# Splitting fp32 weights in two: every fourth low part from an accumulating DMA

## The chip, the core and the metric

The kernel runs on one core of a Trainium2 chip. The core has five engines with a queue of instructions each: TensorE (PE, matrix products), VectorE (DVE), ScalarE (ACT), GpSimd (POOL) and SyncE (SP, used here to issue DMAs). They meet only through semaphores. On-chip memory (SBUF) has 128 partitions; matrix products land in PSUM. Sixteen DMA engines move data between the chip's main memory and SBUF; SP, ACT and POOL can all issue transfers to them.

The metric is the device time of one execution in microseconds (us), the median over runs. The profile is of one execution of its own.

## The reference, cut to what matters

Two layers of an encoder, all in float32, on 256 positions of width 2048. Layer 0 mixes by pooling and attention, layer 1 by a matrix memory (mLSTM); each is followed by a gated feed-forward network with a convolution over positions:

```
for layer in range(DEPTH):
    h = rms_norm(x, norm_mix[layer])
    mixed = ...   # projections of h, pooling | attention, or mLSTM, output projection
    x = x + mixed
    x = x + conv_ffn(rms_norm(x, norm_ffn[layer]), w_up[layer], ..., w_down[layer])

def conv_ffn(x, w_up, conv_w, conv_b, w_down):
    u = x @ w_up                       # 2048 x 11264
    u = c[0] * up[:, :-2] + c[1] * up[:, 1:-1] + c[2] * up[:, 2:] + conv_b
    gate, val = jnp.split(u, 2, axis=-1)
    return (jax.nn.silu(gate) * val) @ w_down   # 5632 x 2048
```

Nearly all the work is products of activations with large weights, each weight used once.

## The kernel before, in words

All weights are laid out on the host as 768 chunks of 128 partitions x 1024 fp32 (512 KB) in the order in which they are used: 48 for the projections into layer 0's mixer, 32 for its output projection (chunks 48 to 79), 264 for the first feed-forward network (80 to 343), 160 for layer 1's mixer (344 to 503), 264 for the second feed-forward network.

TensorE multiplies in a fast format (`F32R`) that keeps fewer bits than fp32. To keep the accuracy, each operand is held as a high part, rounded to that format, and a low part, the rest; a product is three matmuls: high x high, low x high and high x low. `Stream` brings the weights. `load` (line 73) takes a buffer of the pool `wraw` (tag `w`, six buffers) and issues a DMA on SP. `split` (line 81) takes a buffer of the pool `wsplit` (tag `hl`, four buffers, each holding both parts), lets ScalarE cast the chunk into the high part (line 86) and VectorE subtract the high part from the chunk for the low part (line 87). `ahead` (line 91) runs loads `la` chunks and splits `sa` chunks ahead of the chunk that TensorE uses, 5 and 2 here; `next` hands a split chunk to the matmuls. A buffer comes free when its last reader is done: a raw one after the subtraction, a split one after TensorE's last matmul on the chunk.

`stat_group` (line 273) makes one group: 16 or fewer tiles of the inner dimension, four to a chunk, each tile with two matmuls of 512 columns (both parts of the activations against the high part) and two of 256 columns (the low part), all through line 188. In a feed-forward layer `up` makes a group of four chunks for each of 44 column tiles. The group leaves PSUM by a copy on ScalarE (line 321) and an addition on VectorE (322), then goes through a multiply on POOL (821), the convolution and the gate on ScalarE and VectorE (825 to 834). After some of these (4, then 8 each time) `down` makes eight groups of one or two chunks, and POOL adds each into `x` (842). PSUM holds two groups at a time.

What sets the order: TensorE's instructions stay as written in the mixers and in the last down stage; attention heads and the like are woven between projection matmuls by the list `Weave`. On the other engines, and outside the parts marked `manual_schedule`, a planner with its own model of durations orders each engine's queue and inserts the waits. An engine works its queue strictly in order, so an instruction that waits holds all behind it.

At the start the eight pieces of `x` and the first chunks are issued in turn on SP (lines 174 to 177), and the first projection (`kproj`) runs with `st.sa` at 1.

Of the kernel before, what the change touches and what calls it, by code (L numbers as in the profile page):

```python
# [9 lines left out]
F32 = mybir.dt.float32  # L10
F32R = mybir.dt.float32r
AF = mybir.ActivationFunctionType
ALU = mybir.AluOpType
# [3 lines left out]
P = 128  # L17
# [16 lines left out]
CH = 8  # L34
# [29 lines left out]
class Stream:  # L64
# [16 lines left out]
    def split(self):  # L81
        i = self.n_split
        w, n = self.w.pop(i)
        hl = self.spool.tile([P, 2, CH * P], F32R, tag="hl", name=f"hl{i}")
        for c in range(0, CH * P, n):
            self.nc.scalar.copy(hl[:, 0, c : c + n], w[:, c : c + n])  # L86
            self.nc.vector.tensor_sub(hl[:, 1, c : c + n], w[:, c : c + n], hl[:, 0, c : c + n].bitcast(F32))  # L87
        self.hl[i] = hl
        self.n_split += 1

    def ahead(self, i, split=None):
        n = len(self.srcs)
        while self.n_load < min(n, i + self.la + 1):
            if self.n_load >= self.n_split + self.la - self.sa + 1:
                self.split()
            self.load()
        while self.n_split < min(n, i + (self.sa if split is None else split) + 1):
            self.split()
# [54 lines left out]
def trunk(ctx: ExitStack, tc: tile.TileContext, xT, call, catt, cml, wgate, weights, out):  # L153
    nc = tc.nc
    v, a, g, pe = nc.vector, nc.scalar, nc.gpsimd, nc.tensor

    def pool(name, bufs, **kw):
        return ctx.enter_context(tc.tile_pool(name=name, bufs=bufs, **kw))
# [1 line left out]
    cp = pool("const", 1)  # L160
    xp = pool("xres", 1)
    actp = pool("act", 1)
    wp = pool("wraw", 6)
    sp = pool("wsplit", 4)
    smp = pool("small", 2)
    sm1 = pool("small1", 1)
    mmp = pool("mm", 2, space=PSUM)
# [2 lines left out]
    cst = cp.tile([P, NC_ALL], F32, tag="call", name="cst")  # L170
    xg = xp.tile([P, NG + KT * S], F32, tag="x", name="x")
    x = xg[:, NG:].rearrange("p (k s) -> p k s", k=KT)
    st = Stream(nc, wp, sp, weights, 5, 2)
    for i in range(8):
        c0, c1 = NG + 2 * i * S if i else 0, NG + 2 * (i + 1) * S
        nc.sync.dma_start(xg[:, c0:c1], xT[:, c0:c1])
        st.n_load < 5 and st.load(2 if i == 0 else 1)

    wv = Weave()
    ident = cst[:, C_ID : C_ID + P]  # L180
# [115 lines left out]
    def mov_group(act, name, width=512, before=None, after=None):  # L296

        ps = mmp.tile([P, 2, width], F32, tag="mm", name=name)
        per = CH * P // width
        hl = None  # L300
        for k in range(KT):
            if k % per == 0:
                before and before(k)
                hl = st.next()
                after and after(k)
            src = act(k)
            c = (k % per) * width
            for t in range(2):
                xh, xl = src[:, 0, t * P : t * P + P], src[:, 1, t * P : t * P + P]
                o = ps[:, t, :]  # L310
                first, last = k == 0 and (width == 512 or t == 0), k == KT - 1 and (width == 512 or t == 1)
                mm(o, xh, hl[:, 0, c : c + width], first, False)
                mm(o, xh, hl[:, 1, c : c + width], False, False)
                mm(o, xl, hl[:, 0, c : c + width], False, last)
            wv.tick(1.29 * width / 512)
        return ps
# [26 lines left out]
    def attention_layer(norm, nxt):  # L343
        with ExitStack() as es:
# [197 lines left out]
            with tc.manual_schedule(engines={mybir.EngineType.Activation, mybir.EngineType.DVE}):  # L542
                norm.parts(0)
                st.ahead(0, 0)
                norm.parts(1)
                st.sa = 1
                ps = mov_group(xx, "kproj", 512, ahead)
                st.sa = 2
            norm.squares(tp)
            nc.sync.dma_start(cst[:, :C_CONV], call[:, :C_CONV])  # L550
            kc = tp.tile([P, A_PW], F32, tag="rot", name="katt")
# [333 lines left out]
    norms = [Norm(0), None]  # L885
    norms[1] = Norm(1)
    attention_layer(norms[0], norms[1])
    norms.append(Norm(2))
    ffn_layer(0, norms[1], norms[2])
# [169 lines left out]
```

## Time and profile before

| | |
|---|---|
| median of 3 runs | 2225.88 us (2225.22 to 2228.11) |
| the profiled execution, its own time | 2225.61 us |
| its span in the profile | 2223.8 us |
| TensorE busy | 2213.5 us (100% of the span) |
| VectorE busy | 1695.5 us (76%) |
| ScalarE busy | 1213.1 us (55%) |
| POOL busy | 350.1 us (16%) |
| DMA engines, queue of SP | 58.5% of sixteen engines |

A row of the costliest groups reads: line, engine, operation, what it writes and reads with shapes, how often | busy time in us, mean duration in ns | idle time of the engine just before, and who ended it. A row of waits reads: the waiting engine and line, for whom, us in total, how often, the longest. A row of the timeline reads: start, duration, engine, line, operation, and in brackets the idle time before it with its releaser. A row of the stages reads: the stretch, its length, then each engine's busy time with its count of instructions, TensorE's clock as a share of full speed, the share of the DMA engines, GB/s. A row of the chain reads: start, duration, what ran.

### The profile page before, as it was taken

The page shows a single profiled execution, that of the slowest core. Times are in us where ns is not written, and L with a number is a line of the kernel's source. Part 1 is how long each engine was busy: PE and PEld are TensorE (multiplying, and loading weights), DVE is VectorE, ACT ScalarE, POOL GpSimd, SP SyncE. Part 2 cuts the span into 40 slices and gives each one's busy share as a digit, 9 for nine tenths or more (in the row PEclk, how much of TensorE's full clock was granted, in tenths as well). Part 3 has the DMA queues.
Part 4 walks back from the last instruction along what each step waited for, and adds up shares of the span by engine and source line. Part 5 has one row for each costly group of instructions (what it writes and reads, how often), then busy time and mean ns, then how long its engine had stood idle before and what let it go on. Part 6 is the DMA issues. An engine that isn't in the chain of part 4 may idle for free.

```text
span 2223.8 us, 32734 instructions
## 1 busy us (share of the span) xinstructions
PE 2213.5 (100%) x12530; PEld 1925.3 (87%) x12530; DVE 1695.5 (76%) x2099; ACT 1213.1 (55%) x1766; POOL 350.1 (16%) x277
## 2 busy tenths in 40 slices
PE   9999999999999999999999999999999999999999
PEld 7888888888888888888888889888888888888888
DVE  8677777777787777886776676778787778777776
ACT  6666565555554545565555554556555555454553
POOL 1013211312111121251000000221131211112120
PEclk9999999999999999999999999999999999999999
DMA  8545656565666656555566555665655666665664
GB/s 294 163 154 161 195 182 189 182 189 187 191 186 192 189 190 189 184 189 169 179 193 186 183 179 167 188 188 184 189 180 190 190 190 189 190 189 190 189 189 143
DMA packets 116703, 413.50 MB, mean 186 GB/s; under 512 B 12954, under 2 KB 15426, under 8 KB 116546
## 3 DMA queue, kind: packets, MB, share of 16 engines
q1 hardware_dynamic: 113616, 407.96, 58.5%
q10 hardware_dynamic: 2930, 3.45, 0.7%
q8 instruction: 98, 1.61, 0.3%
q14 instruction: 59, 0.48, 0.1%
HBM read 409.22 MB, written 2.14 MB: 185 GB/s over the span
## 4 chain that ended last, share of the span: by engine, by line
PE 97%; DVE 1%; ACT 1%; DMA 1%; issue 0%; SPq 0%; DVEq 0%
PE up L188 44%; PE dn L188 21%; PE op L188 8%; PE mk L188 4%; PE mq L188 4%; PE mo L188 4%; PE mv L188 4%; PE qproj L188 3%; PE vproj L188 1%; DMA w<-in_a_in 1%; DVE hl L87 1%; PE qk L188 1%; PE av L188 1%; PE pool L188 0%; PE ov L188 0%
## 5 line engine op out<-in xcount | busy, mean ns | idle before, releaser
L87 DVE TENSOR_TENSOR hl<-w,hl 128x1024 fp32r<-128x1024 f32 (+1 forms) x769 | 1107.4, 1441 | 298.2 <-ACT hl L86 287.3
L86 ACT CAST hl<-w 128x1024 fp32r<-128x1024 f32 (+1 forms) x769 | 807.8, 1051 | 606.6 <-PE up L188 254.3
L188 PE MATMUL up<-xx,hl 128*128 128x512 f32 (+1 forms) x5632 | 983.7, 337 | 0.0
L188 PEld LDWEIGHTS up<-xx,hl 128*128 128x128 f32 x5632 | 856.8, 188 | 125.2
L188 PE MATMUL dn<-g,hl 128*128 128x512 f32 x2784 | 488.5, 337 | 3.7 <-DVE tb_dn L322 3.7
L188 PEld LDWEIGHTS dn<-g,hl 128*128 128x128 f32 x2784 | 425.1, 189 | 66.2 <-issue 4.0
L821 POOL TENSOR_TENSOR tb_up<-tb_up,R 128x512 f32<-128x512 f32 x88 | 115.5, 1313 | 846.5 <-DVE tb_up L322 831.6
L842 POOL TENSOR_TENSOR x<-x,tb_dn 128x512 f32<-128x512 f32 x88 | 136.0, 1547 | 293.5 <-DVE tb_dn L322 293.5
L321 ACT COPY tb_dn<-dn 128x512 f32<-128x512 f32 x95 | 55.7, 586 | 135.0 <-PE dn L188 133.3
L321 ACT COPY tb_up<-up 128x512 f32<-128x512 f32 x88 | 51.6, 586 | 128.2 <-PE up L188 128.2
L322 DVE TENSOR_TENSOR tb_dn<-dn,tb_dn 128x512 f32<-128x512 f32 x95 | 65.4, 688 | 72.0 <-ACT tb_dn L321 72.0
L322 DVE TENSOR_TENSOR tb_up<-up,tb_up 128x512 f32<-128x512 f32 x88 | 60.8, 691 | 67.3 <-ACT tb_up L321 67.0
L825 ACT ACTIVATE y<-tb_up,cst 128x256 f32<-128x256 f32 x176 | 96.1, 594 | 0.0
L188 PE MATMUL op<-cat,hl 128*128 128x512 f32 (+1 forms) x512 | 92.8, 339 | 0.6 <-DVE cat L537 0.5
L188 PE MATMUL mk<-xx,hl 128*128 128x512 f32 (+1 forms) x512 | 92.5, 338 | 0.0
L188 PE MATMUL mq<-xx,hl 128*128 128x512 f32 (+1 forms) x512 | 92.0, 337 | 0.0
L188 PE MATMUL mo<-hl,xx 128*128 128x512 f32 (+1 forms) x480 | 91.6, 348 | 0.0
L188 PEld LDWEIGHTS op<-cat,hl 128*128 128x128 f32 x512 | 79.2, 188 | 12.5 <-DVE cat L537 1.0
L188 PE MATMUL op<-mcat,hl 128*128 128x512 f32 (+1 forms) x512 | 89.9, 337 | 0.0
L188 PEld LDWEIGHTS mq<-xx,hl 128*128 128x128 f32 x512 | 79.3, 188 | 11.7
L188 PE MATMUL mv<-hl,xx 128*128 128x512 f32 x384 | 89.3, 391 | 0.0
L188 PEld LDWEIGHTS mk<-xx,hl 128*128 128x128 f32 x512 | 79.1, 188 | 11.4
(219 smaller groups left out, 1560.0 us busy)
## 6 DMA issues: line engine op xcount, KB each, us to landing
w<-in_up SPq DMA_DIRECT2D x352, 512.0 KB, 4.2
w<-in_dn SPq DMA_DIRECT2D x176, 512.0 KB, 4.2
w<-in_m_in SPq DMA_DIRECT2D x128, 512.0 KB, 4.0
w<-in_a_in SPq DMA_DIRECT2D x47, 512.0 KB, 4.1
w<-in_a_out SPq DMA_DIRECT2D x32, 512.0 KB, 3.6
w<-in_m_out SPq DMA_DIRECT2D x32, 512.0 KB, 4.3
G<-gd ACTq DMA_DIRECT2D x16, 128.0 KB, 5.2
x<-in_xT SPq DMA_DIRECT2D x7, 256.0 KB, 6.9
```

Source lines behind the costliest of these rows:

```text
L86: self.nc.scalar.copy(hl[:, 0, c : c + n], w[:, c : c + n])
L87: self.nc.vector.tensor_sub(hl[:, 1, c : c + n], w[:, c : c + n], hl[:, 0, c : c + n].bitcast(F32))
L188: pe.matmul(out_, lhsT, rhs, start=start, stop=stop, skip_group_check=True)
L321: a.copy(tb, ps[:, :, 1, :])
L322: v.tensor_add(tb, ps[:, :, 0, :], tb)
L821: g.tensor_mul(u, u, bc(norm.R, 2))
L825: a.activation(y[:, j, :], u[:, j, :], AF.Identity, scale=cw(tl, 1), bias=cw(tl, 3))
L842: g.tensor_add(xs, xs, u)
```

## The change

From chunk 67 on, every fourth chunk (`i % 4 == 3`) is split in another way, 176 chunks in all. ScalarE casts the whole chunk into the high part as before. ScalarE then writes the negated high part into the place of the low part. POOL issues a DMA that reads the chunk from main memory a second time and adds it to what stands there, which leaves chunk minus high part. The raw buffer of such a chunk is free after the cast. VectorE has no part in it.

The depths change for all chunks: splits run three chunks ahead in place of two, loads six in place of five; the split pool has five buffers in place of four, and the raw pool four in place of six, which takes the same 56 KB of each partition. At the start four chunks rather than five are issued between the pieces of `x`.

```diff
@@ split
         w, n = self.w.pop(i)
         hl = self.spool.tile([P, 2, CH * P], F32R, tag="hl", name=f"hl{i}")
-        for c in range(0, CH * P, n):
+        by_dma = i % 4 == 3 and i > 64
+        if by_dma:
+            self.nc.scalar.copy(hl[:, 0], w)
+            self.nc.scalar.activation(hl[:, 1], hl[:, 0].bitcast(F32), AF.Copy, scale=-1.0)
+            self.nc.gpsimd.dma_start(hl[:, 1], self.srcs[i], accum_op=ALU.add)
+        for c in range(0, 0 if by_dma else CH * P, n):
             self.nc.scalar.copy(hl[:, 0, c : c + n], w[:, c : c + n])
             self.nc.vector.tensor_sub(hl[:, 1, c : c + n], w[:, c : c + n], hl[:, 0, c : c + n].bitcast(F32))
@@ trunk
-    wp = pool("wraw", 6)
-    sp = pool("wsplit", 4)
+    wp = pool("wraw", 4)
+    sp = pool("wsplit", 5)
...
-    st = Stream(nc, wp, sp, weights, 5, 2)
+    st = Stream(nc, wp, sp, weights, 6, 3)
...
-        st.n_load < 5 and st.load(2 if i == 0 else 1)
+        st.n_load < 4 and st.load(2 if i == 0 else 1)
@@ attention_layer
                 ps = mov_group(xx, "kproj", 512, ahead)
-                st.sa = 2
+                st.sa = 3
```

## The prediction

> **What bounds the kernel now.** I read the page first: busy times, queues, the chain of work that ended last, and the two groups that the change touches.
>
> ```profile
> span 2223.8 us, 32734 instructions
> ...
> PE 2213.5 (100%) x12530; PEld 1925.3 (87%) x12530; DVE 1695.5 (76%) x2099; ACT 1213.1 (55%) x1766; POOL 350.1 (16%) x277
> ...
> q1 hardware_dynamic: 113616, 407.96, 58.5%
> ...
> PE 97%; DVE 1%; ACT 1%; DMA 1%; issue 0%; SPq 0%; DVEq 0%
> ...
> L87 DVE TENSOR_TENSOR hl<-w,hl 128x1024 fp32r<-128x1024 f32 (+1 forms) x769 | 1107.4, 1441 | 298.2 <-ACT hl L86 287.3
> L86 ACT CAST hl<-w 128x1024 fp32r<-128x1024 f32 (+1 forms) x769 | 807.8, 1051 | 606.6 <-PE up L188 254.3
> ...
> L821 POOL TENSOR_TENSOR tb_up<-tb_up,R 128x512 f32<-128x512 f32 x88 | 115.5, 1313 | 846.5 <-DVE tb_up L322 831.6
> L842 POOL TENSOR_TENSOR x<-x,tb_dn 128x512 f32<-128x512 f32 x88 | 136.0, 1547 | 293.5 <-DVE tb_dn L322 293.5
> ...
> w<-in_up SPq DMA_DIRECT2D x352, 512.0 KB, 4.2
> ```
>
> TensorE is busy for 2213.5 of 2223.8 us, so 10.3 us is all that it ever stands idle. "Busy" in this view can hide stretching, so I looked next at the pace of its work in the chain, in two stages of the first feed-forward layer.
>
> ```profile
> 421.13 89.17 PE up L188 x512
> 510.31 44.59 PE dn L188 x256
> ```
>
> Both stages run at 174 ns per matmul (89.17/512 and 44.59/256), without a break. A chunk of weights feeds 16 matmuls, so a chunk lasts 2.787 us and an up group of four chunks 11.15 us. Last come TensorE's own waits, and stages of the run that hold them.
>
> ```profile
> PE dn L188 <- DVE tb_dn L322: 3.7, 2, 1.8
> PE wps L212 <- DVE warm L207: 1.5, 1, 1.5
> PE ptr L447 <- ACT pr L438: 0.6, 1, 0.6
> PE kproj L188 <- DVE hl L87: 0.6, 1, 0.6
> PE op L188 <- DVE cat L537: 0.5, 1, 0.5
> ```
>
> ```profile
> 0.00:30.00 30.00, 27.83 (x108) 22.21 (x109) 25.11 (x42) 23.62 (x40) 5.45 (x12) 1.00 0.93 350
> 405.00:1000.00 595.00, 594.60 (x3405) 518.67 (x3406) 466.93 (x498) 321.43 (x443) 125.50 (x90) 1.00 0.60 188
> 1482.00:1627.00 145.00, 143.17 (x823) 124.86 (x822) 115.11 (x148) 84.45 (x120) 22.80 (x18) 1.00 0.59 186
> 2131.00:2224.00 93.00, 89.59 (x515) 78.03 (x513) 63.55 (x63) 40.08 (x49) 13.86 (x10) 0.99 0.49 159
> ```
>
> A row gives the stretch, then busy time of PE, PEld, DVE, ACT and POOL, then clock, DMA share and GB/s. In the long feed-forward stretch TensorE loses 0.4 us of 595. Only once, for 0.6 us at the start, did a matmul wait for a split. The time that VectorE spends splitting is thus hidden everywhere after the start, and taking it away can win next to nothing. The question is whether what replaces it stays hidden too.
>
> **The change, part by part.** All sums go against the profiled execution's own 2225.6 us (its span plus 1.8 us around it), 0.3 us below the median of 2225.88.
>
> Removed: 176 subtractions (every fourth chunk from 67 to 767) at the mean of 1441 ns, 254 us of VectorE, which falls from 76% to 65%. Worth nothing on the path, by the waits above.
>
> Added on ScalarE: 176 passes that write the negated high part. The nearest row is the cast of the same size, 1051 ns; 185 us, ScalarE from 55% to 63%. Cover by stage: one up group.
>
> ```profile
> 699.89 0.59 ACT L321 COPY tb_up<-up 128x512 f32<-128x512 f32 x1 [1.79 <-PE up L188]
> 700.37 1.05 ACT L86 CAST hl<-w 128x1024 fp32r<-128x1024 f32 x1
> 701.28 1.29 POOL L821 TENSOR_TENSOR tb_up<-tb_up,R 128x512 f32<-128x512 f32 x1 [9.85 <-DVE tb_up L322]
> 701.46 3.47 DVE L87 TENSOR_TENSOR hl<-w,hl 128x1024 fp32r<-128x1024 f32 x2 [0.26 <-ACT hl L86]
> 703.58 1.09 ACT L825 ACTIVATE y<-tb_up,cst 128x256 f32<-128x256 f32 x2
> 706.36 0.41 ACT L831 ACTIVATE s<-y 128x256 f32<-128x256 f32 x1
> 709.15 0.40 ACT L833 CAST g<-s 128x256 fp32r<-128x256 f32 x1
> 710.98 0.58 ACT L321 COPY tb_up<-up 128x512 f32<-128x512 f32 x1 [1.44 <-PE up L188]
> ```
>
> From evacuation to evacuation there are 11.1 us; ScalarE works 0.59 + 4 x 1.05 + 1.09 + 0.41 + 0.40 = 6.7 us of them, and 7.7 us after. It fits; nothing on the path.
>
> Added on POOL and the DMA engines: 176 accumulating transfers of 512 KB. This is the term that decides. With five split buffers, the buffer of chunk j is free when TensorE has left chunk j-5, and the chunk is due four chunks later: 4 x 2.787 = 11.15 us. In the changed order of ScalarE's instructions stand the cast, the 0.40 us cast of `g`, and the negation: 1.05 + 0.40 + 1.05, and 0.3 us for handovers (0.26 us is such a gap above), 2.8 us. The transfer, from issue to landing, has the remaining 8.4 us. POOL is free to issue it: its multiply in the group above came after 9.85 us of idleness. Behind the waiting issue on POOL stands that multiply of the group just ending, or in the down stages an addition into `x`; both are due after the negation has run.
>
> How long is the transfer? No row shows one with two sources, none issued from POOL. The nearest:
>
> ```profile
> L87 DVE TENSOR_TENSOR hl<-w,hl x769: 693/1226/2317, 5.1 to 2211.4; 128x1024 fp32r<-128x1024 f32 x192, 128x512 fp32r<-128x512 f32 x1
> ...
> DMA to landing us min/median/max: 2.9/4.1/8.7
> ```
>
> ```profile
> 10.00:20.00 10.00, 9.58 (x42) 1.00 1.03 414
> ```
>
> A plain load of the same bytes lands in 2.9 to 8.7 us, 4.1 in the median. At full load the engines moved 414 GB/s, so 512 KB more to read is 1.27 us. [...] Low end 2.9; high end 8.7 + 2 x 1.27 (read and shared engines) + 1.5 = 12.7; I take 4.1 + 1.27 + 1.3 = 6.7, since most loads sit at the median. That is 1.7 us inside 8.4: hidden. If the cover is gone, each microsecond beyond 8.4 costs 176 us, up to (12.7 - 8.4) x 176 = 757 us. [...]
>
> DMA share: 176 x 2 x 1.27 = 447 us, 20% of the span, on top of 58.5%: below the 1.03 seen at full load.
>
> Moved: the depths. A raw buffer now comes back after four chunks, and the load that SP issues then has 11.15 - 1.05 - 1.44 = 8.7 us until its own split is due. At 4.2 us it is covered; the 8.7 us worst case touches a split that itself is one chunk (2.787 us) earlier than before. Nothing. For the start I looked at the chain there.
>
> ```profile
> 15.24 8.09 DMA w<-in_a_in
> ```
>
> SP's queue changes there: the fifth load waits for the first split and stands behind the last pieces of `x`, and the sixth stands behind three constant transfers, 128 + 512 + 362 KB, 2.5 us at 414 GB/s. DMA is the limit in this stretch, and TensorE loses 2.2 us of 30 already. Ends: -0.6 (the `kproj` wait goes) and +4 (those 2.5 us and one more load of 1.27); I take +1.5, as part of the 2.5 is slack.
>
> The two waits of `dn` for `tb_dn` (3.7 us) are in the short first down stage, one chunk per evacuation, where ScalarE now has two negations per layer in front of evacuations: from -3.7 to +4 x 1.05; I take 0.
>
> Outside the feed-forward layers 44 chunks go by DMA, between ScalarE work that is less regular:
>
> ```profile
> ACT hl L86 <- PE mo L188: 36.4, 21, 3.3
> ```
>
> A cast that begins 3.3 us late would miss by 1.6 us: from 0 to 44 x 1.6 = 70 us. I take 1 us, as 3.3 is the longest of 21.
>
> Sum: 2225.6 + 0 + 0 + 1.5 + 0 + 1 = 2228.1, which is +0.1%.
>
> **The rivals.** *The transfer is late* (slower). Place: the first low-part matmul of every fourth chunk; it decides from 8.4 us on. At 9.5 us it gives 1.1 x 176 = 194 us, 2420 us. For it: the 8.7 us row shows what a busy queue does, and two sources double the traffic. Against: 4.1 in the median.
>
> [...]
>
> *Scattered stalls outside the feed-forward layers.* Half of the 44 chunks miss by 1.6 us: 35 us, 2263 us. Against: no matmul there waited for a split before, but their cover shrinks.
>
> *Faster.* VectorE's relief ends the `dn` waits (3.7) and the start the `kproj` wait (0.6), with 1 us more from the deeper splits: 2220.3 us. Against: the `dn` waits end on a chain through ScalarE, which gets more work.
>
> That the change does not do what it says is excluded: the changed order has 176 DMA issues on POOL and 176 fewer subtractions.
>
> **How the numbers follow.** A measurement here tells about 0.2% (4.5 us) from no change. Hidden, as summed: 0.45, its own range 2222 to 2233, of which 0.37 within 0.2% and 0.08 slower. Late transfer 0.27, starved descriptors 0.10, scattered stalls 0.12 (0.01 of it within 0.2%), all slower. Faster rival 0.06 (0.01 within). So faster 0.05, same 0.39, slower 0.56. Though slower holds more chance in all, its cases lie far apart, and the hidden one is the likeliest: 2228 us. The range is 2220 to 2430: it leaves out about 0.02 below and about 0.15 above, the late transfers beyond 9.6 us.
>
> **What the changed profile would show.** Right: no TensorE wait for DMA in the feed-forward stages, up stages still at 89.17 us per 512 matmuls, landings of the POOL transfers under 8.4 us, VectorE near 65%, ScalarE near 63%. Wrong: "PE up waited for DMA hl" some hundred times, up stages longer by the excess times eight groups. The forecast falls if the transfer lands after 8.4 us, or if POOL is busy for microseconds with each issue.

## The result and the profile after

The changed kernel takes 2239.7 us (median of 3 runs, 2239.39 to 2242.12) against 2225.88: a ratio of 1.0063, with a 95% interval of 1.0040 to 1.0086. It is slower by 0.63%, 13.8 us. The profiled execution of after is the slowest of its three, 2242.12 us; its span is 2240.0 us, 16.2 us more than the span of before. The page of after, with the groups and the transfers that the prediction spoke of:

```profile
span 2240.0 us, 33078 instructions
...
PE 2220.1 (99%) x12530; PEld 1927.3 (86%) x12530; DVE 1477.0 (66%) x1923; ACT 1387.7 (62%) x1942; POOL 500.5 (22%) x453
...
q1 hardware_dynamic: 113616, 407.96, 55.4%
q0 software_dynamic: 25344, 92.29, 24.7%
...
L88 ACT ACTIVATE hl<-hl 128x1024 fp32r<-128x1024 f32 x176 | 186.0, 1057 | 2.5
...
hl<-in_up POOLq DMA_DIRECT2D x88, 512.0 KB, 7.2
```

VectorE fell to 66%, ScalarE rose to 62%, the negation takes 1057 ns, and a transfer takes 7.2 us from issue to landing. All that is near the forecast. TensorE, however, now stands idle for 19.9 us (2240.0 - 2220.1) and not 10.3, and is busy for 6.6 us more with the same matmuls (2220.1 against 2213.5). Its waits (engine, for whom, us in total, how often, the longest) and two stages:

```profile
PE kproj L193 <- ACT xx L234: 3.9, 1, 3.9
PE dn L193 <- DVE tb_dn L327: 3.5, 2, 1.8
PE mv L193 <- DMA hl<-in_m_in: 3.1, 5, 1.1
PE qk L193 <- ACT hl_k L675: 1.6, 1, 1.6
...
PE qk L193 <- DVE hl_k L676: 0.7, 1, 0.7
...
PE op L193 <- DMA hl<-in_m_out: 0.4, 1, 0.4
PE mq L193 <- DMA hl<-in_m_in: 0.3, 1, 0.3
```

```profile
405.00:1000.00 595.00, 593.13 (x3404) 517.07 (x3404) 398.27 (x446) 374.50 (x497) 169.46 (x141) 1.00 0.85 234
1000.00:1106.00 106.00, 101.63 (x536) 85.80 (x535) 64.09 (x124) 62.55 (x84) 18.64 (x18) 0.98 0.76 213
```

In the long feed-forward stretch TensorE loses 1.9 us of 595, although 53 of the 176 transfers fall into it; 1.8 of these are one wait of `dn` for `tb_dn` that before has too (there it ends at 405.4 us, so that only 0.4 of it falls into the stretch). In the 106 us at the start of layer 1's mixer it loses 4.4. New waits stand out: one for `xx` at the very start, two for `hl_k` at the first mLSTM head, and some for the new transfers in the mLSTM layer. I laid the matmuls of the two traces side by side, one by one in their order, to see where the distance between them grows. It grows by 5.3 us at the start (`kproj`, below), by 4.2 at the first `qk`, and by 6.1 in eight steps of 0.4 to 1.4 us, each where a low part from a DMA lands late: five in `mv`, one each in `op`, `mq` and `up`. That is 15.6 of the 16.2 us. Each trace also has one stretch of 3.41 us at half clock (0.50) behind a wait of `dn`, from 406.9 us in before and from 1642.0 in after; each costs 1.5 to 1.6 us, and they cancel.

**The start.** The first projection's matmuls, before and then after (shortest, median and longest in ns, then the first and the last start):

```profile
L188 PE MATMUL kproj<-hl,xx x96: 387/389/988, 5.6 to 29.5; 128*128 128x512 f32 x96
```

```profile
L193 PE MATMUL kproj<-hl,xx x96: 387/389/987, 5.6 to 34.8; 128*128 128x512 f32 x96
```

They begin together and end 5.3 us apart. ScalarE's order at that place, before and then after, from the timeline:

```profile
6.02 1.40 ACT L229 ACTIVATE xx<-x 128x256 fp32r<-128x256 f32 x3
...
8.06 1.05 ACT L86 CAST hl<-w 128x1024 fp32r<-128x1024 f32 x1
9.01 0.91 ACT L229 ACTIVATE xx<-x 128x256 fp32r<-128x256 f32 x2
```

```profile
8.23 1.04 ACT L91 CAST hl<-w 128x1024 fp32r<-128x1024 f32 x1 [0.62 <-DMA w<-in_a_in]
...
10.31 1.04 ACT L91 CAST hl<-w 128x1024 fp32r<-128x1024 f32 x1 [0.51 <-DMA w<-in_a_in]
11.27 2.90 ACT L234 ACTIVATE xx<-x 128x256 fp32r<-128x256 f32 x7
```

Before, the next pieces of the activation `xx` come right behind chunk 0's cast, at 6.02. After, the casts of chunks 1 and 2, each waiting for its load, stand ahead of them, and `xx` comes at 11.27. The cause is in `ahead`: before a load it splits when `n_load` has reached `n_split + la - sa + 1`, which at the start (`n_split` is 0) is 4 both before and after (5 - 2 + 1, 6 - 3 + 1). But with `la` at 6, and with four chunks loaded so far in place of five, the one call ahead of this place issues three more loads, not one, and must split three chunks to do so. This part is scheduled by hand, so ScalarE keeps that order. The stages show a second cost (stretch, length, five busy times, clock, DMA share, GB/s):

```profile
10.00:15.00 5.00, 3.15 (x7) 2.05 (x8) 4.75 (x10) 4.69 (x10) 0.00 (x0) 0.54 1.04 410
15.00:20.00 5.00, 5.00 (x19) 4.03 (x18) 5.00 (x8) 4.75 (x9) 2.06 (x2) 0.78 1.04 419
```

TensorE's granted clock is 0.54 and then 0.78 here; before, both stretches had 1.00. It is 0.50 in two stretches of 3.41 us from 10.4 to 17.2 us. The first begins when TensorE has been idle for 2.4 us; in before such a stretch follows one of the two waits of 1.8 us of `dn` (0.50 from 406.9 to 410.3 us) and none follows the other. How much idleness it takes, these runs do not show.

**The first mLSTM head.** The gate rows are stored to main memory (`gd`) and gathered back (`G`), both issued from ScalarE's queue. Before, and then after:

```profile
1041.90 0.54 ACTq L650 DMA_DIRECT2D gd<-gr  x1
1043.76 0.36 ACTq L688 DMA_DIRECT2D G<-gd  x1
```

```profile
1048.67 0.55 ACTq L655 DMA_DIRECT2D gd<-gr  x1
1055.21 0.83 ACTq L693 DMA_DIRECT2D G<-gd  x2
1056.08 0.62 ACT L675 CAST hl_q<-tb_q 128x512 fp32r<-128x512 f32 x1 [3.71 <-DMA gd<-gr]
```

The gather waits for the 40 KB store: 1.86 us before, 6.54 after, and ScalarE stands still with it. At that time the transfer of chunk 359 is under way (issued at 1046.74, landed at 1055.58), and beside it two loads that SP issued 0.4 us apart:

```profile
1046.61 0.81 SPq L77 DMA_DIRECT2D w<-in_m_in  x2
```

Of the 4.2 us at `qk`, 2.3 are the two waits for `hl_k`; most of the rest is another 3.41 us at half clock (0.50) behind them, from 1068.5.

**The late low parts.** The eight steps have more than one cause. The largest, 1.4 us in `mv`, belongs to a transfer that lands quickly, in 5.6 us, but is issued late (chunk 347). Between its cast and its negation ScalarE waits for an addition into `x` on POOL; ScalarE and then POOL:

```profile
1006.22 0.51 ACT L234 ACTIVATE xx<-x 128x256 fp32r<-128x256 f32 x1 [2.96 <-POOL x L847]
...
1007.65 1.04 ACT L88 ACTIVATE hl<-hl 128x1024 fp32r<-128x1024 f32 x1
```

```profile
1008.99 0.88 POOL L89 DMA_DIRECT2D hl<-in_m_in  x1 [0.19 <-issue]
```

From the start of its cast to the issue 6.8 us pass, against 2.6 in the median of the 176. The next transfer (chunk 351) stands for 1.5 us behind a small operation on POOL and then takes 10.1 us to land. The other six land in 8.4 to 10.0 us. The landing goes, in after, with the loads that a transfer meets: with no load issued between 2 us before it and 1 us behind it the median is 5.6 us (12 transfers), with one 7.2 (128), with two 7.5 (33), with three 9.5 (3).

### The profile page after: what moved, and what is told of

Same layout as the page of the kernel before. It is cut to its first block, busy times and chain, and to the rows that moved or that the text cites. A ratio compares the mean times of both kernels' runs of the same rounds, so it can differ in the third digit from the quotient of the medians.

```text
span 2240.0 us, 33078 instructions
## 1 busy us (share of the span) xinstructions
PE 2220.1 (99%) x12530; PEld 1927.3 (86%) x12530; DVE 1477.0 (66%) x1923; ACT 1387.7 (62%) x1942; POOL 500.5 (22%) x453
## 3 DMA queue, kind: packets, MB, share of 16 engines
q1 hardware_dynamic: 113616, 407.96, 55.4%
q0 software_dynamic: 25344, 92.29, 24.7%
## 4 chain that ended last, share of the span: by engine, by line
PE 90%; DMA 3%; issue 3%; DVE 2%; ACT 1%; POOL 0%; SPq 0%; ACTq 0%; POOLq 0%; DVEq 0%
PE up L193 43%; PE dn L193 19%; PE op L193 7%; PE mo L193 4%; PE mk L193 4%; PE mq L193 4%; PE qproj L193 3%; DMA hl<-in_m_in 2%; PE kproj L193 1%; PE vproj L193 1%; PE mv L193 1%; DVE hl L92 1%; PE av L193 1%; ACT hl L91 0%; PE pool L193 0%
## 5 line engine op out<-in xcount | busy, mean ns | idle before, releaser
L92 DVE TENSOR_TENSOR hl<-w,hl 128x1024 fp32r<-128x1024 f32 (+1 forms) x593 | 891.5, 1505 | 169.9 <-ACT hl L91 162.6
L91 ACT CAST hl<-w 128x1024 fp32r<-128x1024 f32 (+1 forms) x593 | 622.7, 1051 | 355.5 <-PE up L193 180.0
L87 ACT CAST hl<-w 128x1024 fp32r<-128x1024 f32 x176 | 184.7, 1050 | 240.2 <-PE up L193 128.3
L89 POOL DMA_DIRECT2D hl<-in_up x88 | 77.4, 880 | 643.5 <-ACT hl L88 633.3
L88 ACT ACTIVATE hl<-hl 128x1024 fp32r<-128x1024 f32 x176 | 186.0, 1057 | 2.5
L839 DVE TENSOR_TENSOR g<-s,g 128x256 fp32r<-128x256 f32 x88 | 38.6, 438 | 122.5 <-ACT g L838 122.5
L89 POOL DMA_DIRECT2D hl<-in_m_in x32 | 27.9, 873 | 280.9 <-ACT hl L88 222.1
```

The source lines that it names most:

```text
L87: self.nc.scalar.copy(hl[:, 0], w)
L88: self.nc.scalar.activation(hl[:, 1], hl[:, 0].bitcast(F32), AF.Copy, scale=-1.0)
L89: self.nc.gpsimd.dma_start(hl[:, 1], self.srcs[i], accum_op=ALU.add)
L839: v.tensor_sub(gt[:, i, 1, :], s_, gt[:, i, 0, :].bitcast(F32))
```

## The experiments

**The depths alone (e_depth).** All chunks are split on VectorE, with five split and four raw buffers:

```diff
-        by_dma = i % 4 == 3 and i > 64
+        by_dma = False
```

> The changed kernel with no chunk split by DMA, and its depths kept (four raw and five split buffers, splits three ahead, loads six). Theory: the loss of 14 us has two parts that are independent; the depths cost only the start, because the splits of chunks 1 and 2 now stand ahead of the second activation tile in ScalarE's order (5.3 us), and the DMA costs the other 9 in the mLSTM stage. Then this kernel runs at 2226 + 5.3 = 2231 us, and its mLSTM stage loses nothing. Rival: the smaller raw pool is what hurts in the mLSTM stage too (loads come in bursts); then this kernel stays near 2238 to 2240 us.

Measured: 2229.87 us, ratio 1.0018 (1.0009 to 1.0027). Of its waits two are long, and only the first is new:

```profile
PE kproj L193 <- ACT xx L234: 4.5, 1, 4.5
PE dn L193 <- DVE tb_dn L327: 3.6, 2, 1.8
```

So the depths cost 4.0 us, and the start is the only place where its matmuls fall behind those of before; the transfers cost the other 9.8 (2239.7 - 2229.87). Matmul for matmul its start ends 5.9 us late, and 1.6 us come back because the half clock that before has at 406.9 us is missing here. The price of the start varies with the half clock that follows it: this lasted 6.8 us in after, here and in e_onesrc, whose `kproj` ends 5.3 to 5.9 us late, and 3.4 us in e_noml, e_negfirst, e_qk and e_half (4.3 to 4.7 us late), all with the same order on ScalarE.

**No transfers in the mLSTM layer (e_noml).** 136 of the 176 transfers stay:

```diff
-        by_dma = i % 4 == 3 and i > 64
+        by_dma = i % 4 == 3 and i > 64 and not 344 <= i < 504
```

> The changed kernel with the DMA splits left out for chunks 344 to 503 (the mLSTM stage), kept in both feed-forward layers and the first output projection. Theory: the late transfers (6 us in eight places) and the wait of the first head (4 us) lie there and go: 2239.7 - 10 = 2229.7 us, with 1 us or less of waits for transfers in the feed-forward layers. Rival (the extra traffic or the added ScalarE pass slow every stage a little, and it only shows up there): 2236 us or more.

Measured: 2230.08 us, ratio 1.0021 (1.0012 to 1.0031). It differs from e_depth by 0.2 us, though it has 136 transfers and e_depth none. The only wait of TensorE for a transfer that its list shows:

```profile
PE up L193 <- DMA hl<-in_up: 0.2, 1, 0.2
```

So outside the mLSTM layer the accumulating transfer is hidden but for 0.2 us, as forecast; its 40 chunks in the mLSTM layer cost 9.6 us.

**ScalarE's order at the start (e_start).** Only chunk 0 is split ahead of `xx`; the loads keep the changed order:

```diff
+                st.la, st.sa = 4, 0
                 st.ahead(0, 0)
+                st.la = 6
```

> The changed kernel with only chunk 0 split ahead of the second activation tile at the start, as before the change; the order of SP's loads stays the changed one (the fifth load behind all of x, the sixth behind the constants). Theory (order on ScalarE): TensorE's 3.9 us wait for the activation tile goes and the first projection ends near 30 us, 2239.7 - 5.3 = 2234.4 us. Rival (order of the loads on SP, the step priced in the prediction): the start stays at 35 us and the time at 2239 to 2240 us.

Measured: 2238.05 us, ratio 1.0057 (1.0040 to 1.0074): between the two expectations. Its runs reach from 2235.47 to 2240.50 us, further apart than the 1.7 us between the medians, so the gain is read in the trace. Its span is 2235.2 us, 4.8 below that of after. The wait for `xx` is gone, the clock is 1.00 from 5 to 20 us, and another wait has grown in its place:

```profile
PE kproj L193 <- DVE hl L92: 3.0, 4, 1.5
```

Matmul for matmul `kproj` now ends 2.3 us behind before and not 5.3. What stays goes with SP's order: before, the sixth load was issued at 10.07 us and landed at 17.02; here it stands behind the constants, goes out at 12.72 and lands at 19.63, and ScalarE's cast waits 0.9 us for it. No run moves the constants, so this part rests on the trace alone.

**The transfer without the second source (e_onesrc).** A plain copy, which leaves out the addition, so the low part is the whole chunk:

```diff
-            self.nc.gpsimd.dma_start(hl[:, 1], self.srcs[i], accum_op=ALU.add)
+            self.nc.gpsimd.dma_start(hl[:, 1], self.srcs[i])
```

> The changed kernel with the POOL transfer as a plain copy of the chunk that does not add to what stands in the buffer: the low part is then the whole chunk, so the products are others than the kernel's. Theory: the second source is what doubles each packet (327 against 159 ns), so packets fall to about 160 ns, and the landing falls from 7.2 us by about 2 us to some 5.3 us; then no matmul in the mLSTM stage waits for a transfer, 2234 to 2236 us. [...]

Measured: 2232.74 us in a single run, below the 2234 to 2236 expected. The same packets and bytes, and their landing:

```profile
q0 software_dynamic: 25344, 92.29, 12.9%
...
hl<-in_up POOLq DMA_DIRECT2D x88, 512.0 KB, 4.8
```

TensorE waits for no transfer any more. The packets take 182 ns in the mean (0.129 x 2230.6 x 16 / 25344) against 349 ns with the addition (0.247 x 2240.0 x 16 / 25344). So the addition costs 2.4 us of the landing (7.2 - 4.8), and POOL as the issuer does not make it long: with a plain copy it is 4.8 us, and the loads from SP land in 4.6 us in after.

**The negation first (e_negfirst).** ScalarE negates the raw chunk, the transfer goes out, and the cast follows:

```diff
-            self.nc.scalar.copy(hl[:, 0], w)
-            self.nc.scalar.activation(hl[:, 1], hl[:, 0].bitcast(F32), AF.Copy, scale=-1.0)
+            self.nc.scalar.activation(hl[:, 1], w, AF.Copy, scale=-1.0)
             self.nc.gpsimd.dma_start(hl[:, 1], self.srcs[i], accum_op=ALU.add)
+            self.nc.scalar.copy(hl[:, 0], w)
```

> The changed kernel with two lines swapped: ScalarE writes the negation first, straight from the raw chunk (scale -1, rounded to the same type), the transfer is issued, and the cast of the high part comes behind it. The transfer goes out one ScalarE operation (1.06 us) earlier: 1.6 to 1.8 us after the split buffer is free in place of 2.81. Theory (the residual stalls at block boundaries are transfers that land up to 1.42 us after they are due, because too little of the 11.15 us is left behind the cast and the negation): the eight late landings (6.06 us of the span in the changed kernel) shrink to under 0.5 us, the start (+5.3) and the first mLSTM head (+4.2) stay, and the median goes from 2239.7 to about 2234 (2232 to 2236). Rival (a transfer issued earlier only lies longer behind the same loads and lands at the same moment, so that landing goes from 7.2 to about 8.3 us): the late landings stay and the median is 2238 to 2241.

Measured: 2236.64 us, ratio 1.0044 (1.0027 to 1.0061), between the two. Each theory had half of it. The waits of `mv` and `op` for DMA are gone; one of `mq` has grown to 2.4 us. And the landing became longer (all transfers, shortest, median and longest), after and then here:

```profile
DMA to landing us min/median/max: 5.4/7.2/10.1
```

```profile
DMA to landing us min/median/max: 5.4/8.9/10.2
```

One group of this kernel shows what changed: cast, transfer, the next load on SP.

```profile
602.39 1.03 ACT L89 CAST hl<-w 128x1024 fp32r<-128x1024 f32 x1
...
602.78 0.88 POOL L88 DMA_DIRECT2D hl<-in_up  x1 [6.97 <-ACT hl L87]
...
603.45 9.00 SPq L77 DMA_DIRECT2D w<-in_up  x4
```

The cast frees the raw buffer, and the load that waited for it goes out at 603.45, 0.7 us behind the transfer. In the changed kernel the cast comes before the negation, so that load is ahead of the transfer (1.5 us, same group), and the next only 4.05 us behind it (transfer at 603.09, loads from 607.14). Over the 132 feed-forward transfers the time that loads took on the sixteen engines while a transfer was under way rose from 3.2 to 4.6 us, the landing from 7.2 to 9.0 (medians). What was won at the issue is lost to the load that it meets.

**The one transfer beside the gate rows (e_qk).**

```diff
-        by_dma = i % 4 == 3 and i > 64
+        by_dma = i % 4 == 3 and i > 64 and i != 359
```

> The changed kernel with one of its 176 transfers undone: chunk 359 alone, the one that is under way when the gate rows are stored to DRAM and gathered back ahead of the first mLSTM head, has its low part subtracted on VectorE as before. Theory (the 40 KB store of the gate rows lies behind the 4 KB accumulating packets of that transfer, and ScalarE, whose queue issues the gather behind a wait for the store, stands 3.7 us with hl_q behind it): from the store's issue to the gather's issue 1.9 us, as before the change (1.86), in place of 6.54; ScalarE's wait of 3.7 us and the 4.2 us at the first qk products vanish, and the median goes from 2239.7 to about 2235.5 (2234 to 2237). Rival (the first head is late because the cast and the negation of chunk 363, 2.1 us, stand ahead of the copy of tb_k on ScalarE): 2 us or more of the 4.2 us stay, the median is 2237.5 or more.

Measured: 2236.49 us, ratio 1.0049 (1.0034 to 1.0064); 3.2 us below after, 1 us less than the 4.2 expected. Store and gather:

```profile
1047.93 0.54 ACTq L655 DMA_DIRECT2D gd<-gr  x1
1049.70 0.36 ACTq L693 DMA_DIRECT2D G<-gd  x1
```

The round trip is 1.77 us, and no wait for `hl_k` is left, so without that one transfer the store is not held up. But the transfer does not act alone. In after the two loads beside it are 0.4 us apart; here the loads of that time are 3.5 us apart (1045.88 and 1049.39), and the store's first packet comes 0.84 us after its issue, against 4.46 in after. And in e_onesrc, with a plain copy and the same pair of loads, the round trip is 4.42 us:

```profile
1046.49 0.55 ACTq L655 DMA_DIRECT2D gd<-gr  x1
...
1050.91 0.84 ACTq L693 DMA_DIRECT2D G<-gd  x2
```

So the addition makes up some 2.1 of the 6.54 us; how the rest divides between the transfer and the loads beside it, no run shows. The rest of the gain went to the next transfer in the row, which now is late by more:

```profile
PE mq L193 <- DMA hl<-in_m_in: 1.8, 1, 1.8
```

**The depths of before under the transfers (e_sa2).** Six raw and four split buffers, five loads and two splits ahead:

```diff
-    wp = pool("wraw", 4)
-    sp = pool("wsplit", 5)
+    wp = pool("wraw", 6)
+    sp = pool("wsplit", 4)
...
-    st = Stream(nc, wp, sp, weights, 6, 3)
+    st = Stream(nc, wp, sp, weights, 5, 2)
...
-        st.n_load < 4 and st.load(2 if i == 0 else 1)
+        st.n_load < 5 and st.load(2 if i == 0 else 1)
...
-                st.sa = 3
+                st.sa = 2
```

> The changed kernel with the depths of the kernel before: six raw and four split buffers, five loads and two splits ahead. The accumulating transfers stay as they are. The split buffer is then free three chunks ahead of its use and not four: 3 x 2.787 = 8.36 us, less 2.81 us up to the issue leaves 5.55 us, against landings of 7.2 us (median). Theory (the time is decided by issue to due against landing, and the fifth split buffer is what hides the transfer): PE waits 1.1 to 1.7 us at each of the 176 chunks, 190 to 300 us in all, and the time is 2420 to 2530. Rival (landing is set by how much load traffic is under way, and stretches only because there is time for it; with PE waiting it falls to the least seen, 5.4 us): almost no waits, 2235 to 2260.

Measured: 2418.15 us in a single run, 192 us more than before: just under the 2420 to 2530 that the budget rule gives, and far from its rival. The longest waits:

```profile
PE dn L193 <- DMA hl<-in_dn: 44.7, 39, 2.4
PE up L193 <- DMA hl<-in_up: 38.1, 40, 3.4
PE mv L193 <- DMA hl<-in_m_in: 16.0, 7, 2.9
PE mk L193 <- DMA hl<-in_m_in: 12.7, 7, 5.2
```

The landing itself is no different (`up` 7.3 us in the median). The waits are not spread as the rule has it: all waits for transfers together are some 124 us at little over 100 places, not 1.1 us or more at each of 176. TensorE's busy time grew by another 66 us (2279.6 us); a mean granted clock of 0.985 accounts for some 36 of them (0.015 x 2416), and what the others are stays open. The fifth split buffer, with splits one chunk further ahead, is what hides the transfer.

**The three repairs together (e_best)**: the edits of e_negfirst, e_start and e_qk.

> The changed kernel with three repairs together: the negation first, only chunk 0 split ahead of the second activation tile at the start, and chunk 359 left to VectorE. Theory (start, first head and late landings are all there is of the loss, and they are separate): of the start about 2.3 of its 5.3 us stays, the 4.2 us of the first head and some 5.5 us of late landings go, and the median is 2227 to 2230, on the level of the kernel before (2225.9) plus the start. Rival (the three are not separate, or 176 transfers at 80 per cent of the DMA engines' time also cost in ways spread too thin to be seen as waits): 2232 to 2237. Neither expects it below 2225.

Measured: 2229.62 us, ratio 1.0018 (1.0008 to 1.0027), within the 2227 to 2230 of the theory. Matmul for matmul the start holds 1.7 of 4.6 us; the rest is small stalls of at most 0.9 us, some of them new in `up`, so a little is spread thinly after all. That the losses are quite separate is not shown: alone the three repairs won 3.1, 1.7 and 3.2 us, 7.9 in all, and together 10.1. Each of them alone left another transfer that TensorE waited for longer (`mq` 2.4 us in e_negfirst and 1.8 in e_qk, `mv` 4.0 in e_start).

**The negation first in the mLSTM layer alone (e_mix)**, otherwise as e_best. In the other layers the cast is first; the negation there still reads the raw chunk:

```diff
+            ml = 344 <= i < 504
+            ml or self.nc.scalar.copy(hl[:, 0], w)
             self.nc.scalar.activation(hl[:, 1], w, AF.Copy, scale=-1.0)
             self.nc.gpsimd.dma_start(hl[:, 1], self.srcs[i], accum_op=ALU.add)
-            self.nc.scalar.copy(hl[:, 0], w)
+            ml and self.nc.scalar.copy(hl[:, 0], w)
```

> As e_best, but the negation stands first only in the 40 chunks of the mLSTM layer; in the other layers the cast is first again, as in the changed kernel. Theory (negation first delays the cast, the cast frees the raw buffer, and so the next plain load is issued 0.66 us behind the transfer instead of 1.4 us ahead of it and 4.2 us behind it, and shares its way: 9.0 us from issue to landing in e_best against 7.2 in the changed kernel): the FFN landings go back to a median of 7.1 to 7.4 us, the mLSTM ones stay as in e_best, the small waits in the FFN layers of e_best (0.87, 0.77, 0.41 us) mostly go, and the median falls from 2229.6 to 2227 to 2229. Rival (the landing was longer because the transfer was issued at another moment against the matmuls, whatever loads): the landings stay near 9 us where the issue is early and fall only by the 1.1 us of the later issue, to 7.9 us or more, with the median at 2229.5 to 2231.

Measured: 2229.71 us, ratio 1.0015 (1.0005 to 1.0025), the same as e_best. The landing in `up`:

```profile
hl<-in_up POOLq DMA_DIRECT2D x88, 512.0 KB, 7.7
```

7.7 us lies between the two expectations. My edit had not put the raw buffer's release back where it was: the negation still reads the raw chunk, so the load goes out 0.3 us ahead of the transfer (1811.38 against 1811.65 in one group), not 1.5. The landings follow when the load meets the transfer, 7.2, 7.7 and 9.1 us in `up` with the load 1.5 us ahead, 0.3 ahead and 0.7 behind; that is three points, not a proof, though the count of loads in after's own trace points the same way. Only 0.2 us of waiting for a transfer is left in this kernel, and it is still no faster than before.

**Twice as many transfers (e_half).**

```diff
-        by_dma = i % 4 == 3 and i > 64
+        by_dma = i % 2 == 1 and i > 64
```

> The changed kernel with every second chunk from a transfer in place of every fourth, 352 in all. In the changed kernel the accumulating transfers took 24.7 per cent of the DMA engines' time and the loads 55.4; twice as many make 49 + 55 = 105 per cent. Theory (the engines' busy time is work that has to be done, the second read makes the packets longer): the DMA engines become the bound, PE waits for low parts throughout, and the time is at least 1.05 x 2240 = 2350, up to 2500; the landing is 9 us or more (median). Rival (packet times are mostly waiting for one another, and there is room left): 2245 to 2300.

Measured: 2271.88 us in a single run; my theory fell, and the time lies in the rival's range.

```profile
q1 hardware_dynamic: 113616, 407.96, 48.8%
q0 software_dynamic: 50688, 184.57, 45.1%
...
hl<-in_up POOLq DMA_DIRECT2D x176, 512.0 KB, 7.9
```

The loads' packets, the same in number and bytes, took 48.8% and not 55.4%, 133 us less of each engine's time (0.554 x 2240.0 - 0.488 x 2270.1): in after not all of that time was work that had to be done, and the 105% that I had added up was no limit here.

## Why the prediction was right or wrong

The direction held the larger chance and came true, and 2239.7 us lies in the range. Both were in good part luck: of the 0.56 for slower 0.27 stood for transfers that are late throughout, which the runs refute, and 0.10 for the case called starved descriptors, of which they show no sign, and the range reached to 2430 for the first of them. What came true is the hidden transfer with losses at other places, and there the forecast number, 2228 us, was 11.7 us too low; 2239.7 lies outside the hidden case's own range of 2222 to 2233.

- *The subtractions are worth nothing*: right. VectorE fell by 218 us of busy time (254 forecast; the subtractions left took 1505 ns in place of 1441), and no wait of TensorE went with it.
- *The negations fit on ScalarE*: right in the feed-forward stages (1057 ns each, 62% in all). At the first mLSTM head ScalarE was late, but for the store, as e_qk shows; at the start of that layer it was late with one negation.
- *The transfer, 8.4 us from issue to due, 6.7 to landing*: right in kind. The budget's 2.8 us ahead of the issue measured 2.81 (median); the landing was 7.2, half a microsecond more. e_noml shows that 136 of the transfers cost 0.2 us, e_sa2 that the budget decides. Of the 132 feed-forward landings two were over 8.4 us, the longest 9.0. That POOL is free, and that ScalarE's negation follows its cast closely, failed where the mLSTM layer begins (chunks 347 and 351). The 1.3 us in the sum of 6.7, and the 1.5 us in its high end, are allowances of mine that no run shows: in their place POOL was busy for 0.88 us with an issue, the first packet came 1.7 us after the issue began, and a landing took 4.8 us with one source and 7.2 with two.
- *The start, +1.5 us*: the step that failed most clearly. It measured +5.3 in the profiled execution (4.0 in e_depth's median). I priced SP's order; what stays when ScalarE's order is restored is 1.7 to 2.3 us (e_best, e_start): a fair size. I did not read what the deeper split did to ScalarE's hand-written order, which cost the other 3 us, the half clock among them.
- *Scattered stalls outside the feed-forward layers, +1 us*: mis-sized. They cost about 10 us (e_noml: 9.6), from 40 chunks. Late casts were the mechanism that I priced, and its like did occur once: the late negation of chunk 347, 1.4 us. The runs showed two others: transfers that meet more loads where one projection ends and the next begins (9.4 to 10.1 us to land, with 5.8 to 6.6 us of the sixteen engines' time taken by loads meanwhile, against 3.2 in the median), and a small store held up behind one transfer and the loads beside it, with ScalarE waiting in line. The rival of scattered stalls (2263) had the place right and the price too high.
- *The `dn` waits, 0*: right, 3.5 us against 3.7.
- *Starved descriptors*, the case in which VectorE's work holds up a transfer that POOL issues: my assumption, and no run shows it. POOL spends 0.88 us on an issue, and the first packet follows 1.7 us (median) after the issue begins. In the traces of seven kernels (after, e_noml, e_negfirst, e_qk, e_sa2, e_best, e_mix) 51 transfers found the engines less than 30% taken by loads until their first packet; in 50 it came after 1.55 to 1.71 us, also where VectorE subtracted for 1.1 us of that time (e_sa2, at 1022.1 us).

The best that the repairs reach is 2229.6 to 2229.7, still above 2225.9: as the waits of before said, there was nothing on VectorE to win.

## What to carry to other kernels

Before moving work from an engine to a DMA, ask which engine waits on the critical one; where the answer is none, there is nothing to win and the move may cost, here 13.8 us. Give such a transfer its budget in time from issue to due, by buffers, and look then at the places where the budget is not the usual one: the start, stage boundaries, and small transfers on which an engine's queue waits. A changed look-ahead also reorders work written out by hand; read that order anew.

## What the runs showed of the hardware that was not expected

- An accumulating transfer's packets took twice as long as plain ones (349 against 182 ns in the mean of all packets of the same queue), and 512 KB landed in 7.2 us against 4.8.
- The 40 KB store that met one accumulating transfer and two loads took 6.5 us in place of 1.9 until its waiter went on, 4.4 with a plain transfer instead, and 1.8 when the transfer was taken away and the loads lay apart.
- POOL was busy for 0.88 us with an issue of an accumulating transfer and for 0.59 with a plain one.
- One wait of 3.9 to 4.7 us on TensorE came with half clock for 6.8 us in three executions and for 3.4 in four; it began, in after, 2.4 us into the wait.
- With twice the transfers the DMA engines' busy share rose from 81% to 95%, the landing only from 7.2 to 7.9 us.
